# Linear attention of a decoder trunk: the small products gathered into fewer visits between the projections, and four dots moved

## The chip, the core and the metric

The kernel runs on one core of one Trainium2 chip. The metric is device time in microseconds (us) of one execution; three executions of the kernel before are on record. The profile is of one further execution.

## The reference

What is computed is a decoder trunk of two layers on 256 tokens of 1024 channels. The first layer mixes tokens by dilated attention, the second by gated linear attention (the part that matters here); both are followed by a convolutional feed-forward part. Every part gets its input through a root-mean-square norm with a shift and a scale that come from a conditioning vector `c`.

```python
mod = jax.nn.silu(c) @ w_ada[i] + b_ada[i]        # 6 pieces of 1024: shifts, scales, gates
...
q, k, gk = chunks(q, B_DK) * (B_DK ** -0.5), chunks(k, B_DK), chunks(gk, B_DK)   # 4 chunks of 64
q_t = q * jnp.exp(bcum)
k_t = k * jnp.exp(-bcum)
k_d = k * jnp.exp(blast - bcum)
A = jnp.where(causal, jnp.einsum('bhncd,bhnsd->bhncs', q_t, k_t), 0.0)
o_intra = jnp.einsum('bhncs,bhnse->bhnce', A, v)
kv = jnp.einsum('bhncd,bhnce->bhnde', k_d, v)
# scan over the chunks: state = decay * state + kv
o = o_intra + jnp.einsum('bhncd,bhnde->bhnce', q_t, s_prev)
o = rmsnorm(o, g_norm)
return (o * jax.nn.silu(r)) @ w_out
```

There are four heads, with 128 channels of q and k and 256 of v each.

## The kernel before, in words

Channels lie on the 128 partitions and the 256 tokens on the free axis, in 8 tiles `h[kt]` of the normed input. TensorE multiplies in a format of reduced precision, so a projection is split: weights come raw from memory (`split`, L169, issued by SyncE into a pool of four buffers that all weight loads share), ScalarE casts the high part `whi` (L176), VectorE subtracts to get the low part `wlo` (L182), and `mm3` (L203 to L205) makes three products of 128x256 for each tile: high by high, high by low, low by high.

In the linear attention (L1211 on) a head is projected by 8 x 2 x 3 = 48 such products into one bank `pqk`. Then come, for each head:

- VectorE: `k_d`, `q_t`, `k_t` (L1233 to L1235), read from `pqk`.
- TensorE: two transposes of `k_d` into `kdt` (L1241), copied by ScalarE to `kdT` (L1242); the scores `a` from `q_t` and `k_t` (L1252), masked by VectorE into `a_t` (L1253).
- TensorE: three chunk sums `kv`, `kdt`, `kv` of `kdT` with the values `v` (L1265, 64 rows each); from them the states st0 (ScalarE, L1272), st1 and st2 (VectorE, L1274).
- TensorE: the output products `o` from `a_t` and `v` (L1291) and from `q_t` and the states (L1294).
- `normed_output`: squares `osq` by ScalarE (L1301), their sum `oacc` by VectorE (L1303), the mean square `ms` by TensorE (L215), its inverse root by ScalarE (L217, L219), and the scaled output `on` by VectorE (L1308).

These small products are in full single precision. Heads follow each other: while one head is projected, the small products of the head before are put between its projection products. Behind the four heads stand the gate projections `pr` (weights `w_r_b`) and the output projection (`w_out_b`).

The tiles `q_t`, `k_t`, `k_d`, `kdT`, `a_t` and the states have two buffers each: those of the third head take the place of those of the first, and may be written only when the first head's last readers are done. `oacc` and `osq` have one.

The modulation `mod` for the second layer is computed meanwhile by VectorE: `next_ada` (L461) loads one piece of `w_ada` (1 MB) into a buffer of the same pool and makes two dots with `c` (L142, two instructions each: the product with its sum, and the reading of the accumulator). The caller may name instructions behind which the dots are to stand.

The order of each engine's queue is made when the program is built, by a scheduler that goes by estimated times and by the statements `behind(...)`, which say that one instruction is to be issued after another on its engine. Each engine then runs its queue strictly in that order. In the code before, the place of most small products among the projection products is left to the scheduler.

Of the kernel before, what the change touches and what calls it, by code (L numbers as in the profile page):

```python
# [18 lines left out]
P = 128  # L19
D = 1024  # L20
T = 256
# [38 lines left out]
def trunk(ctx: ExitStack, tc: tile.TileContext, I, out):  # L60
# [77 lines left out]
    def ada_dot(l, n, s, raw):  # L138
# [3 lines left out]
        i = nc.vector.tensor_tensor_reduce(  # L142
# [20 lines left out]
    last_load, copied, last_lo = [None], [None], [None]  # L163
# [1050 lines left out]
    def states(hd, between=lambda turned: ()):  # L1214
        if hd == 0:
            w = split(I["w_qk_b"][0][:, KT * P :], KT * P)
            pk = bank("pqk", "p")[:, :T]
            pq = early_q
            for kt in range(KT):
                mm3(pk, parts(w, P * kt), h[kt], kt == 0, kt == KT - 1)  # L1220
        else:
            w = split(I["w_qk_b"][hd], 2048, **(dict(low=first_kt[:1], late=first_kt[:1]) if hd == 2 else {}))
            pqk = bank("pqk", "p")
            pq, pk = pqk[:, :T], pqk[:, T:]
            for kt in range(KT):
                mm3(pq, parts(w, 2 * P * kt), h[kt], kt == 0, False)
                mm3(pk, parts(w, 2 * P * kt + P), h[kt], False, kt == KT - 1)
# [5 lines left out]
        nc.vector.tensor_tensor(k_d, pk, e_d[:, c], op=ALU.mult)  # L1233
        nc.vector.scalar_tensor_tensor(q_t, pq, P ** -0.5, e_q[:, c], op0=ALU.mult, op1=ALU.mult)
        first_kt.append(nc.vector.tensor_tensor(k_t, pk, e_k[:, c], op=ALU.mult))  # L1235

        ps = bank("kdt", "t")
        kd = gt([P, T], "kdT", bufs=2)
        for t in range(2):
            c = slice(P * t, P * t + P)  # L1240
            last_kd = nc.tensor.transpose(ps[:, c], k_d[:, c], ident)  # L1241
        nc.scalar.copy(kd, ps[:, :T])  # L1242

        a_t = gt([P, 2, P], "a_t", bufs=2)
        nc.gpsimd.memset(a_t, 0.0)

        def masked(*after):
            pa = bank("a", "st"[hd == 3])
            for t in range(2):
                c = slice(P * t, P * t + P)  # L1250
                with behind(*after):
                    last_a[0] = mm(pa[:, c], k_t[:, c], q_t[:, c], start=True, stop=True)  # L1252
            kept[0] = nc.vector.copy_predicated(a_t, causal.bitcast(U32), pa[:, :T].rearrange("p (a b) -> p a b", a=2))  # L1253

        if hd < 3:
            masked()
# [238 lines left out]
```

## Time and profile before

| | |
|---|---|
| three executions | 756.5, 756.79, 760.47 us, median 756.79 |
| the profiled execution | 757.08 us |
| its span in the trace | 755.3 us |
| mean granted clock of TensorE | 0.998 |
| dots on VectorE (L142) | 96, 114.3 us busy, 1231 ns each |
| transfers | 187.20 MB, mean 248 GB/s |

Times in the trace are counted from the start of the span. A row of the timeline has the start, the busy time, the engine, the line, the operation, out<-in and the count; in brackets stands the idle time of the engine before it and what released it. One product in full precision counts as two in the trace (a row `x4` can be two instructions). Busy times of neighbouring products overlap, so the time that one costs is read from start to start.

### The profile page before, as it was taken

Reading aid. Unit: us, or ns where it says so; the run is one execution under the profiler, and the core shown is the slowest. Engines: PE = TensorE matmul, PEld = TensorE weight load, DVE = VectorE, ACT = ScalarE, POOL = GpSimd, SP = SyncE. Lnnn points to the kernel's source line nnn. Section 1 sums busy time; section 2 is a strip of 40 time slices with the busy share of each in tenths; the row PEclk is TensorE's granted clock in tenths of the full one; section 3 lists DMA queues with packets and bytes.
Section 4 is the critical chain, followed back from the end, with each engine's and each line's share of the span. In section 5 each row is a group of like instructions: output and inputs, shape, how many; then the busy total and the mean of one; then the engine's idle time right before and its main releaser. Section 6 shows DMA issues by size and latency. Waiting matters only on the chain.

```text
span 755.3 us, 16079 instructions
## 1 busy us (share of the span) xinstructions
PE 746.6 (99%) x6416; PEld 730.4 (97%) x6416; DVE 650.1 (86%) x1197; ACT 483.1 (64%) x949; POOL 32.9 (4%) x57
## 2 busy tenths in 40 slices
PE   8999999999999999999999999999999999999997
PEld 6999999999999999999999999999999999999996
DVE  6999998898889689999999778977959999997592
ACT  5567666566566388676767456925868767666551
POOL 0001010101101010000000000000010000000100
PEclk9999999999999999999999999999999999999999
DMA  9989889879877368777556987854547767774621
GB/s 347 400 298 331 279 311 375 290 233 325 291 250 267 99 222 305 280 261 272 190 183 224 347 272 233 330 224 191 200 169 250 291 216 254 210 174 159 206 98 56
DMA packets 39481, 187.20 MB, mean 248 GB/s; under 512 B 9020, under 2 KB 11708, under 8 KB 25838
## 3 DMA queue, kind: packets, MB, share of 16 engines
q1 hardware_dynamic: 39024, 185.73, 70.2%
q8 instruction: 50, 0.82, 0.4%
q10 hardware_dynamic: 382, 0.45, 0.2%
q14 instruction: 25, 0.20, 0.1%
HBM read 185.06 MB, written 1.10 MB: 246 GB/s over the span
## 4 chain that ended last, share of the span: by engine, by line
PE 90%; DVE 5%; ACT 2%; DMA 2%; issue 1%; DVEq 0%; ACTq 0%
PE pab L204 10%; PE pab L203 10%; PE pab L205 10%; PE pqk L203 6%; PE pqk L205 5%; PE pqk L204 5%; PE pd L204 4%; PE pd L203 4%; PE pd L205 4%; PE pv L203 4%; PE pv L205 4%; PE pv L204 4%; PE py L203 2%; PE py L205 2%; PE py L204 2%; PE early L333 1%
## 5 line engine op out<-in xcount | busy, mean ns | idle before, releaser
L176 ACT CAST whi<-raw 128x1024 fp32r<-128x1024 f32 (+4 forms) x264 | 237.8, 945 | 106.9 <-PE pab L204 54.9
L182 DVE TENSOR_TENSOR wlo<-raw,whi 128x1024 fp32r<-128x1024 f32 (+5 forms) x248 | 263.5, 1093 | 32.2 <-ACT whi L176 31.2
L205 PE MATMUL pab<-hhi,wlo 128*128 128x256 f32 x672 | 184.8, 276 | 0.0
L204 PE MATMUL pab<-hlo,whi 128*128 128x256 f32 x672 | 184.7, 277 | 0.0
L203 PE MATMUL pab<-hhi,whi 128*128 128x256 f32 x672 | 182.9, 277 | 0.0
L204 PEld LDWEIGHTS pab<-hlo,whi 128*128 128x128 f32 x672 | 126.0, 188 | 0.2
L205 PEld LDWEIGHTS pab<-hhi,wlo 128*128 128x128 f32 x672 | 126.2, 188 | 0.0
L203 PEld LDWEIGHTS pab<-hhi,whi 128*128 128x128 f32 x672 | 125.0, 188 | 0.1
L142 DVE CUSTOM_DVE_ANT_0 ada_raw<-ada_raw,c_bc 128x1024 f32<-128x1024 f32 x96 | 114.3, 1231 | 4.2 <-DMA ada_raw<-in_w_ada 4.2
L203 PE MATMUL pqk<-hhi,whi 128*128 128x256 f32 x374 | 102.5, 279 | 0.0
L204 PE MATMUL pqk<-hlo,whi 128*128 128x256 f32 x374 | 102.0, 278 | 0.0
L205 PE MATMUL pqk<-hhi,wlo 128*128 128x256 f32 x374 | 101.5, 278 | 0.0
L205 PE MATMUL pd<-ghi,wlo 128*128 128x256 f32 x308 | 84.9, 276 | 0.0
L204 PE MATMUL pd<-glo,whi 128*128 128x256 f32 x308 | 84.9, 276 | 0.0
L203 PE MATMUL pd<-ghi,whi 128*128 128x256 f32 x308 | 84.7, 276 | 0.0
L203 PEld LDWEIGHTS pqk<-hhi,whi 128*128 128x128 f32 x374 | 69.9, 188 | 0.2
L204 PEld LDWEIGHTS pqk<-hlo,whi 128*128 128x128 f32 x374 | 69.9, 188 | 0.0
L205 PEld LDWEIGHTS pqk<-hhi,wlo 128*128 128x128 f32 x374 | 69.2, 188 | 0.7 <-issue 0.7
L205 PEld LDWEIGHTS pd<-ghi,wlo 128*128 128x128 f32 x308 | 57.8, 188 | 0.0
L204 PEld LDWEIGHTS pd<-glo,whi 128*128 128x128 f32 x308 | 57.8, 188 | 0.0
L203 PEld LDWEIGHTS pd<-ghi,whi 128*128 128x128 f32 x308 | 57.7, 188 | 0.0
L204 PE MATMUL pv<-wlo,hhi 128*128 128x384 f32 (+2 forms) x160 | 52.8, 332 | 0.0
(278 smaller groups left out, 1463.6 us busy)
## 6 DMA issues: line engine op xcount, KB each, us to landing
raw<-in_w_up SPq DMA_DIRECT2D x42, 1024.0 KB, 4.9
ada_raw<-in_w_ada SPq DMA_DIRECT2D x29, 1024.0 KB, 5.9
raw<-in_w_down SPq DMA_DIRECT2D x28, 704.0 KB, 4.4
ada_raw<-in_w_ada SPq DMA_DIRECT2D x38, 512.0 KB, 7.0
raw<-in_wqk SPq DMA_DIRECT2D x18, 1024.0 KB, 6.9
raw<-in_wv SPq DMA_DIRECT2D x14, 768.0 KB, 6.5
raw<-in_w SPq DMA_DIRECT2D x7, 960.0 KB, 5.8
raw<-in_w_v_b SPq DMA_DIRECT2D x6, 768.0 KB, 5.7
```

The costliest lines, as they stand in the source:

```text
L142: i = nc.vector.tensor_tensor_reduce(w, w, c_bc, op0=ALU.mult, op1=ALU.add, scale=1.0, scalar=0.0, accum_out=dot,)
L176: copied[0] = nc.scalar.copy(part(hi[:, c]), part(raw[:, c]))
L182: last_lo[0] = nc.vector.tensor_tensor(part(lo[:, c]), part(raw[:, c]), part(hi[:, c].bitcast(F32)), op=ALU.subtract)
L203: mm(ps, a[0], b[0], start=start, stop=False)
L204: mm(ps, a[0], b[1], start=False, stop=False)
L205: return mm(ps, a[1], b[0], start=False, stop=stop)
L333: mm(ps[:, 0 : T + 1], early[:, P * kt : P * kt + P], early_x[kt][:, 0 : T + 1], start=(kt == 0), stop=(kt == KT - 1))
```

## The change

The function `states` is taken apart into its steps (`head`, `project_head`, `scaled_head`, `turned_head`, `masked_head`, `sums_of_head`, `states_of_head`, `products`), and the main sequence now calls the steps in the order in which TensorE is to run them, each behind the one before. Between halves (four of the eight tiles) of the third and fourth heads' projections stand four visits of small products: transposes and scores of the first head; its sums; transposes and scores of the second head; and the second head's sums with the third head's transposes and the first head's output products. The rest follows the fourth head's projection. The two pieces of `w_ada` that were taken behind the first and second gates are now taken together behind the third head's `k_t`, ahead of the fourth head's projection in the program; the second head's st1 and st2 are stated to stand behind their dots.

All 148 rows of TensorE in the stretch from the third head's projection to the gates are the same instructions in another order. The returns from small products to projection products in it go from nine to five. First, TensorE before, in the fourth head's projection (`pqk`); `kv` and `kdt` are the chunk sums of the second head, `o` an output product of the first. The first sum stands by itself:

```order
L204 MATMUL pqk<-hlo,whi 128x256
L1265 MATMUL kdt<-v_6365,kdT 128x256
L205 MATMUL pqk<-hhi,wlo 128x256
...
L205 MATMUL pqk<-hhi,wlo 128x256
L203 MATMUL pqk<-hhi,whi 128x256
L1265 MATMUL kv<-v_6365,kdT 128x256
L1265 MATMUL kv<-v_6366,kdT 128x256
L1294 MATMUL o<-q_t,st_6689 128x64
L204 MATMUL pqk<-hlo,whi 128x256
```

Behind the change (lines of the new code: sums L1280, transposes L1256, output products L1307 and L1310) the three sums stand together at the half of the fourth head, with the third head's transposes and the first head's output products right behind:

```order
L205 MATMUL pqk<-hhi,wlo 128x256
L1280 MATMUL kv<-v_6365,kdT 128x256
L1280 MATMUL kdt<-v_6365,kdT 128x256
L1280 MATMUL kv<-v_6366,kdT 128x256
L1256 MATMUL kdt<-ident,k_d 128x128 x2
L1307 MATMUL o<-a_t,v_6365 128x128
L1310 MATMUL o<-q_t,st_6783 128x64
L1307 MATMUL o<-a_t,v_6366 128x128
L1310 MATMUL o<-q_t,st_6785 128x64
L1310 MATMUL o<-q_t,st_6787 128x64
```

What moved: the sums are in one piece, and all ten output products of the first head, which before were spread over the projection, stand directly behind them. Next, the end of the fourth head's projection after the change. `ms` is the mean square of the first head's output, `a` the third head's scores, the sums those of the third head:

```order
L205 MATMUL pqk<-hhi,wlo 128x256
L215 MATMUL ms<-oacc,ones_d 128x256
L1268 MATMUL a<-q_t,k_t 128x128 x2
L1280 MATMUL kv<-v_6365,kdT 128x256
L1280 MATMUL kdt<-v_6365,kdT 128x256
L1280 MATMUL kv<-v_6366,kdT 128x256
```

Before, `ms` stood behind the third head's sums; now it stands directly behind the last projection product, ahead of them. On VectorE before, around `q_t` of the third head (`q_t_6858`); `st1_6773` is the second head's, `oacc_6790` the first head's. No dot is among these rows; one pair stands directly ahead of them and another some rows further ahead:

```order
L1233 TENSOR_TENSOR k_d_6860<-pqk_6809,e_d_6547 128x256
L1274 SCALAR_TENSOR_TENSOR st2_6691<-st1_6689,dec_6531,kv_6683 128x256
L1274 SCALAR_TENSOR_TENSOR st1_6773<-st0_6771,dec_6553,kdt_6756 128x256
L1274 SCALAR_TENSOR_TENSOR st2_6775<-st1_6773,dec_6553,kv_6767 128x256
L1234 SCALAR_TENSOR_TENSOR q_t_6858<-pqk_6809,e_q_6548 128x256
L1235 TENSOR_TENSOR k_t_6859<-pqk_6809,e_k_6549 128x256
L1303 TENSOR_TENSOR oacc_6790<-osq_6788 128x256
L1233 TENSOR_TENSOR k_d_6944<-pqk_6893,e_d_6547 128x256
```

VectorE after, from `q_t` of the third head (`q_t_6833`), which is the instruction that waits for TensorE's output products of the first head, to `oacc` of the first head (`oacc_6937`):

```order
L1245 SCALAR_TENSOR_TENSOR q_t_6833<-pqk_6737,e_q_6548 128x256
L1246 TENSOR_TENSOR k_t_6834<-pqk_6737,e_k_6549 128x256
L142 ISA ada_raw_6839,dot_6841<-ada_raw_6839,c_bc_97 128x1024
L142 ISA dot_6841 128x1
L142 ISA ada_raw_6839,dot_6845<-ada_raw_6839,c_bc_97 128x1024
L142 ISA dot_6845 128x1
L142 ISA ada_raw_6849,dot_6851<-ada_raw_6849,c_bc_97 128x1024
L142 ISA dot_6851 128x1
L142 ISA ada_raw_6849,dot_6855<-ada_raw_6849,c_bc_97 128x1024
L142 ISA dot_6855 128x1
L1292 SCALAR_TENSOR_TENSOR st1_6889<-st0_6887,dec_6553,kdt_6822 128x256
L1319 TENSOR_TENSOR oacc_6937<-osq_6935 128x256
```

Four dots (eight rows) now stand between `k_t` of the third head and st1 of the second head, and so ahead of the first head's `oacc`. SyncE's queue of loads before and after, from the last weights of q and k on (`w_r_b` are the gate weights):

```order
L169 DMA raw<-in_w_qk_b 128x2048 x3
L169 DMA raw<-in_w_r_b 128x2048
L135 DMA ada_raw<-in_w_ada 128x2048
L169 DMA raw<-in_w_r_b 128x2048
L135 DMA ada_raw<-in_w_ada 128x2048 x2
```

```order
L169 DMA raw<-in_w_qk_b 128x2048 x3
L135 DMA ada_raw<-in_w_ada 128x2048 x2
L169 DMA raw<-in_w_r_b 128x2048 x2
L135 DMA ada_raw<-in_w_ada 128x2048
L169 DMA raw<-in_w_r_b 128x2048
```

Both moved pieces of `w_ada` now stand ahead of the first gate weights.

The diff, with the new functions:

```diff
@@ -139,7 +139,7 @@
-        i = nc.vector.tensor_tensor_reduce(
+        i = dotted[0] = nc.vector.tensor_tensor_reduce(
...
@@ -1211,81 +1211,97 @@
     o_n, first_kt, accs = [], [], []
     last_a, last_sq, copies, kept = [None], [None], [None], [None, None]
 
-    def states(hd, between=lambda turned: ()):
+    heads = [{} for _ in range(4)]
+
+    def head(hd, **kw):
+        y = heads[hd]
         if hd == 0:
-            w = split(I["w_qk_b"][0][:, KT * P :], KT * P)
-            pk = bank("pqk", "p")[:, :T]
-            pq = early_q
-            for kt in range(KT):
-                mm3(pk, parts(w, P * kt), h[kt], kt == 0, kt == KT - 1)
+            y["w"] = split(I["w_qk_b"][0][:, KT * P :], KT * P)
+            y["pq"], y["pk"] = early_q, bank("pqk", "p")[:, :T]
         else:
-            w = split(I["w_qk_b"][hd], 2048, **(dict(low=first_kt[:1], late=first_kt[:1]) if hd == 2 else {}))
+            y["w"] = split(I["w_qk_b"][hd], 2048, **kw)
             pqk = bank("pqk", "p")
-            pq, pk = pqk[:, :T], pqk[:, T:]
-            for kt in range(KT):
-                mm3(pq, parts(w, 2 * P * kt), h[kt], kt == 0, False)
-                mm3(pk, parts(w, 2 * P * kt + P), h[kt], False, kt == KT - 1)
+            y["pq"], y["pk"] = pqk[:, :T], pqk[:, T:]
+
+    def project_head(hd, kts, *after):
+        y = heads[hd]
+        for kt in kts:
+            with behind(*after):
+                if hd:
+                    mm3(y["pq"], parts(y["w"], 2 * P * kt), h[kt], kt == 0, False)
+                    last = mm3(y["pk"], parts(y["w"], 2 * P * kt + P), h[kt], False, kt == KT - 1)
+                else:
+                    last = mm3(y["pk"], parts(y["w"], P * kt), h[kt], kt == 0, kt == KT - 1)
+        return last
+
+    def scaled_head(hd):
+        y = heads[hd]
         part = min(hd, 1)
         e_q, e_k, e_d, dec = gates[part]
         own = hd - PARTS[part][0]
         c = slice(T * own, T * own + T)
         q_t, k_t, k_d = (gt([P, T], nm, bufs=2) for nm in ("q_t", "k_t", "k_d"))
-        nc.vector.tensor_tensor(k_d, pk, e_d[:, c], op=ALU.mult)
-        nc.vector.scalar_tensor_tensor(q_t, pq, P ** -0.5, e_q[:, c], op0=ALU.mult, op1=ALU.mult)
-        first_kt.append(nc.vector.tensor_tensor(k_t, pk, e_k[:, c], op=ALU.mult))
-
-        ps = bank("kdt", "t")
-        kd = gt([P, T], "kdT", bufs=2)
+        nc.vector.tensor_tensor(k_d, y["pk"], e_d[:, c], op=ALU.mult)
+        nc.vector.scalar_tensor_tensor(q_t, y["pq"], P ** -0.5, e_q[:, c], op0=ALU.mult, op1=ALU.mult)
+        first_kt.append(nc.vector.tensor_tensor(k_t, y["pk"], e_k[:, c], op=ALU.mult))
+        y.update(q_t=q_t, k_t=k_t, k_d=k_d, dec=dec[:, 4 * own : 4 * own + 4])
+
+    def turned_head(hd, *after):
+        y = heads[hd]
+        y["ps"] = ps = bank("kdt", "t")
+        y["kd"] = kd = gt([P, T], "kdT", bufs=2)
         for t in range(2):
             c = slice(P * t, P * t + P)
-            last_kd = nc.tensor.transpose(ps[:, c], k_d[:, c], ident)
+            with behind(*after):
+                last = nc.tensor.transpose(ps[:, c], y["k_d"][:, c], ident)
         nc.scalar.copy(kd, ps[:, :T])
-
-        a_t = gt([P, 2, P], "a_t", bufs=2)
-        nc.gpsimd.memset(a_t, 0.0)
-
-        def masked(*after):
-            pa = bank("a", "st"[hd == 3])
-            for t in range(2):
-                c = slice(P * t, P * t + P)
-                with behind(*after):
-                    last_a[0] = mm(pa[:, c], k_t[:, c], q_t[:, c], start=True, stop=True)
-            kept[0] = nc.vector.copy_predicated(a_t, causal.bitcast(U32), pa[:, :T].rearrange("p (a b) -> p a b", a=2))
-
-        if hd < 3:
-            masked()
+        y["a_t"] = gt([P, 2, P], "a_t", bufs=2)
+        nc.gpsimd.memset(y["a_t"], 0.0)
+        return last
+
+    def masked_head(hd, *after):
+        y = heads[hd]
+        pa = bank("a", "st"[hd == 3])
+        for t in range(2):
+            c = slice(P * t, P * t + P)
+            with behind(*after):
+                last_a[0] = mm(pa[:, c], y["k_t"][:, c], y["q_t"][:, c], start=True, stop=True)
+        kept[0] = nc.vector.copy_predicated(y["a_t"], causal.bitcast(U32), pa[:, :T].rearrange("p (a b) -> p a b", a=2))
+        return last_a[0]
+
+    def sums_of_head(hd, *after):
+        y = heads[hd]
         vh = slice(T * hd, T * hd + T)
-        st = []
-        ahead = between(last_kd)
         kv = bank("kv", "t")
+        y["d"] = kv[:, :T], y["ps"][:, T:], kv[:, T:]
         for n in range(3):
             t, r = n // 2, slice(CH * (n % 2), CH * (n % 2) + CH)
-            d = (kv[:, :T], ps[:, T:], kv[:, T:])[n]
-            with behind(*ahead):
-                last = mm(d, kd[r, P * t : P * t + P], v[t][r, vh], start=True, stop=True)
-        if hd == 3:
-            masked(last)
+            with behind(*after):
+                last = mm(y["d"][n], y["kd"][r, P * t : P * t + P], v[t][r, vh], start=True, stop=True)
+        return last
+
+    def states_of_head(hd, *after):
+        y = heads[hd]
+        st = []
         for n in range(3):
-            d = (kv[:, :T], ps[:, T:], kv[:, T:])[n]
             s = gt([P, T], f"st{n}", bufs=2)
             if n == 0:
-                copies[0] = nc.scalar.copy(s, d)
+                copies[0] = nc.scalar.copy(s, y["d"][n])
             else:
-                kept[1] = nc.vector.scalar_tensor_tensor(s, st[-1], dec[:, 4 * own + n : 4 * own + n + 1], d,
-                                               op0=ALU.mult, op1=ALU.add)
+                with behind(*after):
+                    kept[1] = nc.vector.scalar_tensor_tensor(s, st[-1], y["dec"][:, n : n + 1], y["d"][n],
+                                                             op0=ALU.mult, op1=ALU.add)
             st.append(s)
-        return q_t, a_t, st
+        y["state"] = y["q_t"], y["a_t"], st
 
     last_o = [None]
 
-    def output(hd, *state):
-        normed_output(hd, products(hd, *state))
-
-    def products(hd, q_t, a_t, st, last=None):
+    def products(hd, *after):
+        q_t, a_t, st = heads[hd]["state"]
         po = bank("o", "s")
         for et in range(2):
             ev = slice(T * hd + P * et, T * hd + P * et + P)
-            with behind(*([last] if last and et else [])):
+            with behind(*after):
                 for t in range(2):
                     d = po[:, T * et + P * t : T * et + P * t + P]
                     mm(d, v[t][:, ev], a_t[:, t, :], start=True, stop=False)
@@ -1330,23 +1346,46 @@
             with behind(*norm_ops[1:]):
                 nc.scalar.activation(r_g[-1], pr, AF.Silu)
 
-    s0 = states(0)
-    s1 = states(1)
-    output(0, *s0)
-    s2 = states(2)
-    po1 = []
-
-    def ahead(turned):
-        po1.append(products(1, *s1, last=turned))
-        return last_o
-
-    s3 = states(3, ahead)
-    normed_output(1, po1[0], last_a)
-    po2 = products(2, *s2)
+    head(0)
+    project_head(0, range(KT))
+    scaled_head(0)
+    head(1)
+    last = project_head(1, range(KT))
+    head(2, low=first_kt[:1], late=first_kt[:1])
+    turned_head(0, last)
+    last = masked_head(0, last)
+    scaled_head(1)
+    last = project_head(2, range(4), last)
+    last = sums_of_head(0, last)
+    states_of_head(0)
+    head(3, low=first_kt[1:2], late=first_kt[1:2])
+    last = project_head(2, range(4, KT), last)
+    turned_head(1, last)
+    last = masked_head(1, last)
+    scaled_head(2)
+    for _ in range(2):
+        next_ada(kept[0], first_kt[2])
+    last = project_head(3, range(4), last)
+    last = sums_of_head(1, last)
+    states_of_head(1, dotted[0])
+    last = turned_head(2, last)
+    po0 = products(0, last)
+    last = project_head(3, range(4, KT), last_o[0])
+    normed_output(0, po0, [last])
+    last = norm_ops[0]
+    scaled_head(3)
+    masked_head(2, last)
+    last = sums_of_head(2, last)
+    states_of_head(2)
+    last = turned_head(3, last)
+    po1 = products(1, last)
+    last = sums_of_head(3, last_o[0])
+    masked_head(3, last)
+    states_of_head(3)
+    normed_output(1, po1, last_a)
+    po2 = products(2)
     gate(0)
-    low_0 = last_lo[0]
-    next_ada(first_kt[1])
-    po3 = products(3, *s3)
+    po3 = products(3)
     normed_output(2, po2, last_o)
     normed_output(3, po3)
 
@@ -1357,7 +1396,6 @@
             for s in range(2):
                 nc.scalar.copy(level[kt][s], h[kt][s])
     gate(1)
-    next_ada(low_0)
     next_ada(accs[2])
     for n in range(4):
 
```

More of the change, by code (lines that the diff above doesn't have):

```diff
@@ L160, in ada_chunk @@
                 ada_dot(l, n, s, raw)
-    last_load, copied, last_lo = [None], [None], [None]
+    last_load, copied, last_lo, dotted = [None], [None], [None], [None]
     def split(src, n, dmas=1, after=((), ()), late=(), low=(), lows=True, view=None):
```

## The prediction

> **What bounds the kernel now.** I read the page first: busy time of the engines, then the shares of the chain that ended last.
>
> ```profile
> PE 746.6 (99%) x6416; PEld 730.4 (97%) x6416; DVE 650.1 (86%) x1197; ACT 483.1 (64%) x949; POOL 32.9 (4%) x57
> PE 90%; DVE 5%; ACT 2%; DMA 2%; issue 1%; DVEq 0%; ACTq 0%
> ```
>
> TensorE (PE) is busy for 99% of the span. So a time saved on PE is a time saved, and a time in which PE waits is added; work elsewhere counts only where PE comes to wait for it. Second, the stretch that the change rewrites, from the projection of the third head to the gates, as busy time by stretch (the columns are the stretch, its length, busy us and counts of PE, PEld, DVE, ACT and POOL, then the granted clock, the DMA share and GB/s).
>
> ```profile
> 491.40:498.20 6.80, 6.80 (x57) 6.29 (x56) 6.80 (x11) 2.18 (x5) 0.00 (x0) 1.00 0.60 226
> 498.20:509.60 11.40, 11.40 (x90) 10.38 (x88) 7.59 (x16) 2.76 (x8) 0.31 (x1) 1.00 0.63 235
> 509.60:518.60 9.00, 9.00 (x69) 7.83 (x67) 6.23 (x14) 5.16 (x9) 0.31 (x1) 1.00 0.00 1
> ```
>
> PE has no gap in these 27.2 us, at the full clock. There is no PE wait here that a better order could remove; only the price of switching between kinds of product can go. VectorE (DVE) has slack: 11.40 − 7.59 = 3.8 us in the second stretch and 2.8 us in the third. Third, what DVE waits for there, by its timeline; the last row has the wait in brackets.
>
> ```profile
> 496.37 1.22 DVE L142 CUSTOM_DVE_ANT_0 ada_raw<-ada_raw,c_bc 128x1024 f32<-128x1024 f32 x1
> 498.66 1.22 DVE L182 TENSOR_TENSOR wlo<-raw,whi 128x1024 fp32r<-128x1024 f32 x1
> 508.43 0.42 DVE L1234 SCALAR_TENSOR_TENSOR q_t<-pqk,e_q 128x256 f32<-128x256 f32 x1 [2.40 <-PE o L1294]
> 508.77 0.41 DVE L1235 TENSOR_TENSOR k_t<-pqk,e_k 128x256 f32<-128x256 f32 x1
> 509.10 0.42 DVE L1303 TENSOR_TENSOR oacc<-osq 128x256 f32<-128x256 f32 x1
> ```
>
> The third row is the most important of all. It is q_t of the third head. That tile has two buffers, so it may be written only after the output products of the first head, its last readers, are done. DVE waited 2.40 us for them with nothing in hand. The dots (one pair began at 496.37, and the next work followed at 498.66, so a pair takes 2.29 us) stood ahead of this wait, where DVE had time to spare.
>
> **The change part by part. (1) Fewer returns to the projection: −1.1.** All 96 projection products and all small products remain; only their order differs. Rows of PE in the stretch (start, busy, line):
>
> ```profile
> 492.02 0.37 PE L203 MATMUL pqk<-hhi,whi 128*128 128x256 f32 x1
> 492.23 0.28 PE L204 MATMUL pqk<-hlo,whi 128*128 128x256 f32 x1
> 492.35 0.28 PE L205 MATMUL pqk<-hhi,wlo 128*128 128x256 f32 x1
> ...
> 501.06 0.28 PE L204 MATMUL pqk<-hlo,whi 128*128 128x256 f32 x1
> 501.27 0.70 PE L1265 MATMUL kdt<-v,kdT 64*128 64x256 f32 x2
> 501.90 0.38 PE L205 MATMUL pqk<-hhi,wlo 128*128 128x256 f32 x1
> 502.12 0.28 PE L203 MATMUL pqk<-hhi,whi 128*128 128x256 f32 x1
> 502.24 0.28 PE L204 MATMUL pqk<-hlo,whi 128*128 128x256 f32 x1
> ```
>
> The first projection product behind a visit takes 0.21 us until the next one starts, against 0.12 in a run of them: a return costs 0.09. The chunk sums of the second head stand in two pieces. The one-product piece occupies PE from 501.18 (501.06 and a regular step of 0.12) to 501.90, and its return takes 0.22 instead of 0.12: 0.72 + 0.10 = 0.82. That the sums in one visit cost no more than the remaining piece of two is read from the first head, whose three stand together:
>
> ```profile
> 495.29 0.28 PE L204 MATMUL pqk<-hlo,whi 128*128 128x256 f32 x1
> 495.50 0.48 PE L1265 MATMUL kv<-v,kdT 64*128 64x256 f32 x1
> ...
> 496.56 0.39 PE L205 MATMUL pqk<-hhi,wlo 128*128 128x256 f32 x1
> ...
> 503.18 0.28 PE L203 MATMUL pqk<-hhi,whi 128*128 128x256 f32 x1
> 503.39 1.13 PE L1265 MATMUL kv<-v,kdT 64*128 64x256 f32 x4
> 504.45 0.43 PE L1294 MATMUL o<-q_t,st 128*128 128x64 f32 x2
> ```
>
> Three of them: 495.29 to 496.56, 1.27. The two left over in the second head: 503.18 to 504.45, 1.27 as well. So the single piece is saved whole, 0.82. In the order of instructions the returns to the projection fall from nine to five; one of the four is in the piece, and three more give 3 × 0.09 = 0.27. Together −1.1. The bounds are 0 (the joined visits put other switches in their place) and −1.5 (each of the four visits saves its way in as well).
>
> **(2) The four dots behind k_t of the third head: +3.6.** Afterwards DVE has, in this order: q_t of the third head (still waiting for the first head's output products), k_t, two pairs of dots, st1 of the second head, oacc of the first. PE now has the output products directly behind the second head's sums, then the second half of the fourth head's projection, and then ms, the mean square made from that oacc. The third head's scores, sums, the output products of the second head and everything behind are queued behind ms. So the chain from the end of the first head's output products to ms decides, and its length comes from these rows and those above:
>
> ```profile
> 508.23 0.39 PE L1241 MATMUL kdt<-ident,k_d 128*128 128x128 f32 x2
> 512.35 0.47 DVE L1274 SCALAR_TENSOR_TENSOR st<-st,dec,kv 128x256 f32<-128x256 f32 x1
> 512.73 0.87 DVE L1308 SCALAR_TENSOR_TENSOR on<-o,small,rstd 128x256 f32<-128x256 f32 x2
> 514.85 0.41 DVE L1235 TENSOR_TENSOR k_t<-pqk,e_k 128x256 f32<-128x256 f32 x1
> 515.46 0.71 PE L1252 MATMUL a<-q_t,k_t 128*128 128x128 f32 x4
> ```
>
> PE left the output products at 508.23 and q_t began at 508.43: 0.20. q_t to k_t 0.34, k_t to the next 0.33. Two pairs of dots 2 × 2.29 = 4.58. st1 0.38 (512.35 to 512.73). oacc 0.42, and from the end of a DVE result to the PE product on it 0.20 (k_t ends at 515.26, the scores start at 515.46). The sum is 0.20 + 0.34 + 0.33 + 4.58 + 0.38 + 0.42 + 0.20 = 6.45 us. In that time PE has 24 projection products. 48 of them ran from
>
> ```profile
> 485.99 0.28 PE L203 MATMUL pqk<-hhi,whi 128*128 128x256 f32 x1
> ...
> 491.44 0.38 PE L1241 MATMUL kdt<-ident,k_d 128*128 128x128 f32 x2
> ```
>
> in 5.45 us, so 24 take 2.72, with the return 2.81. PE stands still for 6.45 − 2.81 = 3.6 us. Without the dots it would not: 6.45 − 4.58 = 1.87 is less than 2.81. The bounds of this stall are 3.0 (the hops shorter, DVE's operations closer together) and 4.0 (st1 or the first squares on ScalarE late by some tenths). DVE waits longer before q_t in turn, since it has no dots to fill that time (2.40 + 4.58, less some 2 us by which the output products come earlier: about 5), but nothing on PE is late for it: q_t and k_t are first needed by the third head's scores, which stand behind ms anyway.
>
> **(3) Loads.** The two ada loads move ahead of the gate weights on SyncE's queue, so the first gate weights take a later slot.
>
> ```profile
> 492.92 0.33 SPq L169 DMA_DIRECT2D raw<-in_w_r_b  x1
> raw<-in_w_r_b SPq DMA_DIRECT2D x4, 1024.0 KB, 6.4
> 532.44 2.00 ACT L176 CAST whi<-raw 128x1024 fp32r<-128x1024 f32 x2
> ```
>
> A slot like that of 492.92 with the median of 6.4 us to landing gives 499.3. ScalarE's casts of 1 us a half stand ahead of its copy of the second head's kdT, which the joined sums need at about 502 to 503. That is hidden; with a landing two us later some tenths would show. I take 0, bounds 0 and +0.3. The third and fourth gate loads start when the dots free their buffers, some 10 us before PE uses them, and stay hidden.
>
> **(4) The tail of the stretch.** The mean square of the third head joins another visit and saves about 0.1, which I leave out; the casts of the first output weights stand behind a table load on ScalarE and shorten a slack of about 2 us there: 0, bound +1.
>
> **The sum.** The profiled execution took 757.08 us (span 755.3): 757.08 − 1.1 + 3.6 = 759.6. It lies 0.29 above the median of the runs shown, 756.79, so the forecast for the median is **759.3 us**, 0.33% above before. The likeliest case's own range, with the bounds of its terms (−1.5 + 3.0 at one end; 0.3 less saved and 4.0 at the other), is 758.3 to 760.0.
>
> **The rivals. (a) The clock falls in the new stall, slower than before.** At the end of the program PE goes idle:
>
> ```profile
> 749.08 0.85 PE L916 MATMUL y<-ident,x_all 128*128 128x128 f32 x6
> 749.00:752.00 3.00, 0.94 (x9) 0.69 (x8) 1.73 (x5) 1.45 (x4) 0.00 (x0) 0.96 0.00 0
> 752.00:755.00 3.00, 0.00 (x0) 0.00 (x0) 0.00 (x0) 0.00 (x0) 0.00 (x0) 0.50 0.45 175
> ```
>
> The last product ends at 749.93. The clock averages 0.96 up to 752 and is 0.50 after it, so it fell (1 − 0.96) × 3.00 / 0.50 = 0.24 us ahead of 752, that is 1.8 us after the last product. A stall of 3.6 us is twice that. What it costs to come back is seen at the start, where the same warming products take 2.08 / 8 = 0.26 us each and later 1.16 / 8 = 0.145:
>
> ```profile
> 6.65 2.08 PE L301 MATMUL warm<-ones_d 128*128 128x128 f32 x8
> 10.64 1.05 PE L301 MATMUL warm<-ones_d 128*128 128x128 f32 x6
> 13.01 1.16 PE L301 MATMUL warm<-ones_d 128*128 128x128 f32 x8
> ```
>
> The slow spell lasts from 6.65 to about 11, at most 4.4 us at about half rate: a loss of at most 2.2; part of it can pass while PE still stands still. I take +1.5, so 760.8, 0.5% slower, with 761.5 as its far end. The place is the small products behind ms, and it decides only if the stall exceeds 1.8 us. Against it speaks that a single fall, at the program's end, is all that these rows hold. The Trainium skill, page "TensorE: Matmul & The Clock Gate", section "What's actually happening", says that the gate falls to half rate after at least one idle window of about 3.4 us, and that windows run freely. By that rule a stall of 3.6 us would seldom hold a whole window, and the sum would stay at 759.3; the row of 1.8 us does not fit a whole idle window, so the trace so far leans the other way. Chance 0.33.
>
> **(b) The dots are hidden.** If ms or oacc does not wait behind the dots (a wait falls elsewhere than I read), only term (1) is left: 756.79 − 1.1 = 755.7. For it: DVE has 3.8 us of slack in the stretch. Against it: that slack lies in waits ahead of q_t, and the dots stand behind it in a queue that runs in order. Chance 0.09.
>
> **(c) The change also stalls the output projection** by using up the slack of part (4): +0.9, so 760.2. Chance 0.08.
>
> **How the numbers follow.** The forecast has the remaining 0.50. The range 758.2 to 761.4 takes in the forecast, (c) and nearly all of (a); outside lie (b) and some of the tail of (a). A measurement of this kernel can tell about 0.5%, 3.8 us, from no change: 753.0 and 760.6 are the borders. Slower than 760.6: two thirds of (a), a quarter of (c) and a few of the forecast's misses, with the unknown size of a lower clock in mind 0.30. Faster than 753.0 would take a gain that no row shows: 0.02. Within: 0.68.
>
> **What would show it.** In the profile after, the waits of PE should have ms waiting for oacc, some 3.6 us, in a stretch that had none; DVE's wait for q_t by the output products should grow from 2.4 to about 5; the four dots should stand back to back behind k_t; the granted clock at the small products behind ms tells forecast from (a). The stretch without its stall should be about 1.1 us shorter. I am wrong if PE has no gap at ms, if the gap is there but shorter than 3 us, or if a new gap appears at the gate weights.

## The result and the profile after

The changed kernel takes 765.58 us (median of six executions, 761.75 to 770.01), against 756.75 us for the kernel before (756.5 to 760.47): a ratio of 1.0109, 95% interval 1.0072 to 1.0146. Measured again beside the experiments on another occasion it took 766.29 us against 757.14 us, 1.0119 (1.0089 to 1.0149). The profiled execution took 765.64 us, its span is 763.8 us.

The page of the changed kernel, first the engines, then the granted clock by slice of 19.1 us:

```profile
PE 752.2 (98%) x6416; PEld 734.9 (96%) x6416; DVE 650.9 (85%) x1197; ACT 483.7 (63%) x949; POOL 33.1 (4%) x57
...
PEclk9999999999999999999999999987999999999999
```

DVE, ACT and POOL have as much to do as before. TensorE has 5.6 us more of busy time for the same instructions, and two slices have a clock under 0.9, where before no slice had. Both lie in the stretch that the change rewrites. The waits of TensorE in it, in one row (us in all, times, longest), and TensorE's timeline there:

```profile
PE ms L215 <- DVE oacc L1319: 3.4, 1, 3.4
```

```profile
504.89 0.56 PE L1310 MATMUL o<-q_t,st 128*128 128x64 f32 x4
505.25 0.37 PE L203 MATMUL pqk<-hhi,whi 128*128 128x256 f32 x1
...
508.05 0.28 PE L205 MATMUL pqk<-hhi,wlo 128*128 128x256 f32 x1
511.69 1.19 PE L215 MATMUL ms<-oacc,ones_d 128*128 128x256 f32 x2 [3.36 <-DVE oacc L1319]
512.68 1.06 PE L1268 MATMUL a<-q_t,k_t 128*128 128x128 f32 x4
...
523.47 1.06 PE L215 MATMUL ms<-oacc,ones_d 128*128 128x256 f32 x2
524.33 0.57 PE L1307 MATMUL o<-a_t,v 128*128 128x128 f32 x2
...
526.30 0.56 PE L1310 MATMUL o<-q_t,st 128*128 128x64 f32 x4
526.66 0.37 PE L203 MATMUL pr<-hhi,whi 128*128 128x256 f32 x1
```

The stall is where the prediction put it: 3.36 us at ms of the first head, for oacc. Behind it every product takes nearly twice its time from start to start until 524 us; by busy time the scores take 1.06 instead of 0.61 and ms 1.19 instead of 0.7. VectorE in the same place:

```profile
499.46 0.44 DVE L1269 COPY_PREDICATED a_t<-causal,a 128x256 f32<-128x256 uint32 x1
505.48 0.42 DVE L1245 SCALAR_TENSOR_TENSOR q_t<-pqk,e_q 128x256 f32<-128x256 f32 x1 [5.59 <-PE o L1310]
505.82 0.41 DVE L1246 TENSOR_TENSOR k_t<-pqk,e_k 128x256 f32<-128x256 f32 x1
506.15 1.22 DVE L142 CUSTOM_DVE_ANT_0 ada_raw<-ada_raw,c_bc 128x1024 f32<-128x1024 f32 x1
...
510.73 0.48 DVE L1292 SCALAR_TENSOR_TENSOR st<-st,dec,kdt 128x256 f32<-128x256 f32 x1
511.13 0.42 DVE L1319 TENSOR_TENSOR oacc<-osq 128x256 f32<-128x256 f32 x1
```

VectorE stands idle for 5.59 us at q_t, and then has 4.58 us of dots (506.15 to 510.73) ahead of the oacc that TensorE waits for. The stretch cut at the places where the clock changes (columns as before: length, busy us of PE, PEld, DVE, ACT and POOL, granted clock, DMA share, GB/s):

```profile
490.70:508.30 17.60, 17.60 (x144) 16.40 (x142) 10.64 (x18) 4.00 (x9) 0.31 (x1) 1.00 0.32 121
508.30:511.05 2.75, 0.03 (x1) 0.00 (x0) 2.75 (x7) 1.07 (x4) 0.00 (x0) 1.00 0.49 140
511.05:511.70 0.65, 0.01 (x1) 0.04 (x1) 0.65 (x3) 0.19 (x1) 0.00 (x0) 0.50 1.07 454
511.70:524.71 13.01, 13.01 (x48) 10.64 (x49) 5.23 (x14) 4.38 (x8) 0.31 (x1) 0.50 0.26 109
524.71:526.66 1.95, 1.95 (x20) 1.95 (x19) 1.95 (x2) 1.95 (x4) 0.00 (x0) 1.00 0.00 0
```

The clock fell to 0.50 at 511.05, 2.7 us after TensorE's last product had ended at 508.33, and came back at 524.71. From the first transpose at the start of the stretch to the first gate product it now takes 526.66 - 490.70 = 35.96 us; before it took 518.59 - 491.44 = 27.15. That is 8.81 us more: 3.4 from the stall and some 6.2 from 13 us of work at half clock, less 0.8 by which the stretch is shorter without a stall (experiments 1 and 8 to 10 size the last two). What lies ahead of the stretch is 0.74 us shorter and what lies behind it 0.5 longer in this execution, which leaves the 8.6 us of the two profiled executions.

### The profile page after: what moved, and what is told of

Its sections match the earlier page's. It is cut to its first block, busy times and chain, and to the rows that moved or that the text cites. A ratio compares the mean times of both kernels' runs of the same rounds, so it can differ in the third digit from the quotient of the medians.

```text
span 763.8 us, 16078 instructions
## 1 busy us (share of the span) xinstructions
PE 752.2 (98%) x6416; PEld 734.9 (96%) x6416; DVE 650.9 (85%) x1197; ACT 483.7 (63%) x949; POOL 33.1 (4%) x57
## 4 chain that ended last, share of the span: by engine, by line
PE 89%; DVE 5%; DMA 3%; ACT 2%; issue 1%; SPq 0%; DVEq 0%; ACTq 0%
PE pab L204 10%; PE pab L203 10%; PE pab L205 10%; PE pqk L203 5%; PE pqk L205 5%; PE pqk L204 5%; PE pd L204 4%; PE pd L205 4%; PE pd L203 4%; PE pv L205 4%; PE pv L203 4%; PE pv L204 4%; PE py L203 2%; PE py L205 2%; PE py L204 2%; DVE ada_raw L142 2%
```

## The experiments

Each experiment is set against the kernel before on the same chip: experiments 1 to 4 on one chip, 5 to 8 on a second, 9 to 11 on a third. Theory A: the four dots hold back oacc, TensorE stands still for it, and in that stall the clock falls; the order of TensorE's products itself is harmless. Rival B: the order itself (small full-precision products packed together) or the earlier loads slow TensorE. Rival C: four dots are too much for this stretch wherever they stand.

**1. The dots ahead of q_t**, TensorE's order and the loads as in the change.

```diff
-    scaled_head(2)
     for _ in range(2):
-        next_ada(kept[0], first_kt[2])
+        next_ada(kept[0], first_kt[1])
+    scaled_head(2)
```

> The new order of TensorE is kept whole; only the four dots are taken ahead of q_t of the third head, into the wait that VectorE has there anyway. Theory A (the dots hold back oacc, TensorE stands still at ms for 3.4 us, and the granted clock falls in that stall): no wait of TensorE at ms, the clock stays at 1.00, and only the saved returns are left: 756.75 - 1.1 = 755.7 us. Rival B (the order itself is to blame: the small full-precision products packed together, or the earlier loads, bring the clock down or slow the products): the time stays near 765 us with no stall.

Measured: 756.15 us against 757.07 us, 0.999 (0.998 to 1.0). On VectorE the dots now fill the wait, and TensorE runs from the projection into ms:

```profile
505.34 0.48 DVE L1292 SCALAR_TENSOR_TENSOR st<-st,dec,kdt 128x256 f32<-128x256 f32 x1
...
506.32 0.42 DVE L1245 SCALAR_TENSOR_TENSOR q_t<-pqk,e_q 128x256 f32<-128x256 f32 x1
...
506.98 0.42 DVE L1319 TENSOR_TENSOR oacc<-osq 128x256 f32<-128x256 f32 x1
```

```profile
508.55 0.28 PE L205 MATMUL pqk<-hhi,wlo 128*128 128x256 f32 x1
508.67 0.59 PE L215 MATMUL ms<-oacc,ones_d 128*128 128x256 f32 x2
```

The last dot ends before st1 at 505.34, oacc is done at 507.40, 1.3 us ahead of ms. Same order on TensorE, same order of loads, no stall, full clock: rival B falls. The stretch takes 26.38 us (491.06 to 517.44), 0.77 less than before: that is what the new order saves there.

**2. One pair of dots ahead of q_t, one behind k_t.**

```diff
+    next_ada(kept[0], first_kt[1])
     scaled_head(2)
-    for _ in range(2):
-        next_ada(kept[0], first_kt[2])
+    next_ada(kept[0], first_kt[2])
```

> One pair of dots ahead of q_t of the third head, the other pair left where the change put both, behind k_t. Theory A: the wait at ms shrinks by one pair, 3.4 - 2.3 = 1.1 us. If the clock falls only when the idle time goes on for over 1.8 us, it stays at 1.00 here, and the time is 755.7 + 1.1 = 756.8 us. If any wait of about 1 us is enough for the clock to fall, half-clock time of one or more spells is added, 758.5 to 763. Rival B: near 765 us.

Measured: 757.81 us, 1.0016 (0.9999 to 1.0033). The wait at ms:

```profile
PE ms L215 <- DVE oacc L1319: 1.1, 1, 1.1
```

3.36 - 2.29 = 1.07 us, as expected: the stall goes with the number of dots ahead of oacc. The clock stayed at 1.00 through it. The median is 1.0 us above the 756.8 expected; the stretch of the profiled execution is 27.55 us, 1.17 more than in experiment 1, so the rest lies outside it and was not followed up.

**3. The stall filled with products of no use.** Eleven small products of a constant tile go into the bank of ms ahead of the real one; they add work and change no result.

```diff
-    def rstd_of(squares, n=D, tag=None):
+    def rstd_of(squares, n=D, tag=None, idle=0):
         ps = bank("ms", tag)
+        for _ in range(idle):
+            mm(ps[:, :P], ones_d, ones_d, start=True, stop=True)
...
-            rr = rstd_of([acc], 256, "s")
+            rr = rstd_of([acc], 256, "s", 11 if hd == 0 else 0)
```

> The changed kernel with its dots where the change put them, plus eleven 128x128 products of a constant tile on TensorE, directly ahead of the ms of the first head and written into the bank that ms then overwrites: about 11 x 0.29 = 3.2 us of work of no use in a stall of 3.4 us. Theory A: ms starts when it did (VectorE is as late as before), but TensorE is not idle, the clock stays at 1.00, and the time is 755.7 + 3.4 = 759.1 us; the difference from the changed kernel, some 6 us, is the price of the clock alone. Rival B: unchanged, near 765 us, with the clock low again.

Measured: 760.03 us, 1.0048 (1.0031 to 1.0066). TensorE idles for 0.81 us instead of 3.36, and ms starts no earlier:

```profile
508.71 2.62 PE L215 MATMUL ms<-ones_d 128*128 128x128 f32 x22
512.14 0.70 PE L217 MATMUL ms<-oacc,ones_d 128*128 128x256 f32 x2 [0.81 <-DVE oacc L1321]
512.68 0.61 PE L1270 MATMUL a<-q_t,k_t 128*128 128x128 f32 x4
```

The scores take 0.61 us again: the clock is full. This separates the two costs. The wait as such is worth 760.03 - 756.15 = 3.9 us by the medians, and 29.78 - 26.38 = 3.4 us by the stretches of experiments 3 (491.24 to 521.02) and 1. The clock is worth 766.29 - 760.03 = 6.3 us in the median of the changed kernel's later measurement; counted from the kernel before on its own chip, 9.15 - 2.96 = 6.2.

**4. Three buffers for q_t**, so that it waits for nobody.

```diff
-        q_t, k_t, k_d = (gt([P, T], nm, bufs=2) for nm in ("q_t", "k_t", "k_d"))
+        q_t, k_t, k_d = (gt([P, T], nm, bufs=3 if nm == "q_t" else 2) for nm in ("q_t", "k_t", "k_d"))
```

> The changed kernel with three buffers for q_t instead of two, nothing else edited. q_t of the third head need not wait for the output products of the first, so q_t, k_t and the four dots start some 5.6 us earlier, and oacc is not late. Theory A: no wait of TensorE at ms, clock at 1.00, 755.7 us, the same as with the dots moved ahead. If instead the dots are too long wherever they stand in this stretch (4.6 us of VectorE's time are not there), a wait of 1 us or more remains at ms or at the third head's products.

Measured: 756.49 us, 0.9988 (0.9976 to 0.9999), with no wait of TensorE in the stretch. The dots stand behind k_t, as in the change, yet start early, since q_t is not held:

```profile
501.30 0.41 DVE L1245 SCALAR_TENSOR_TENSOR q_t<-pqk,e_q 128x256 f32<-128x256 f32 x1
...
502.30 1.22 DVE L142 CUSTOM_DVE_ANT_0 ada_raw<-ada_raw,c_bc 128x1024 f32<-128x1024 f32 x1
...
507.89 0.42 DVE L1319 TENSOR_TENSOR oacc<-osq 128x256 f32<-128x256 f32 x1
```

So the cause has two conditions, the dots and the wait ahead of them: dots behind a waiting instruction cost, the same dots behind one that does not wait do not. Rival C falls.

**5. The kernel before with the dots alone moved**, TensorE's order left to the scheduler.

```diff
             w = split(I["w_qk_b"][hd], 2048, **(dict(low=first_kt[:1], late=first_kt[:1]) if hd == 2 else {}))
+            if hd == 3:
+                for _ in range(2):
+                    next_ada(first_kt[2])
...
-    low_0 = last_lo[0]
-    next_ada(first_kt[1])
...
-    next_ada(low_0)
```

> The kernel before with only the dots moved: both pieces of w_ada behind k_t of the third head, loads ahead of the gate weights as in the change, and TensorE's order left to the scheduler. The scheduler then puts oacc of the first head ahead of the dots and the first head's output products earlier. Theory A (what costs is oacc queued behind dots while ms stands at TensorE's head, not the dots as such): no wait of TensorE over 1 us, clock at 1.00, 756 to 758 us. Rival C (four dots in this stretch or the moved loads are themselves too much): some 3 us of waits and a time over 760 us.

Measured: 755.97 us, 0.9989 (0.9975 to 1.0003), no wait of TensorE in the stretch. The scheduler then puts oacc ahead of the dots by itself, takes the sums of the second head in one visit, and the stretch takes 26.09 us, 0.29 less than with the order stated by hand in experiment 1. It moved a good deal of TensorE's order with the dots, so it shows that the moved dots and loads do no harm there, not what they cost in the old order. It also shows that a stretch as short does not need the new order.

**6. Five products of no use instead of eleven** (the edit of experiment 3 with 5 for 11).

> As the run with eleven products of no use ahead of ms, but five of them: 1.2 us of work, so that TensorE is idle for about 2.2 us in one piece instead of 0.8. It asks how long an idle time lets the clock fall. Without a fall 760.0 us as with eleven. If 1.8 us is enough whatever came before, the clock falls in most executions and the time is 762 to 766 us. If it needs over 2.2 us, or depends on where a free-running window stands, none or a part of the executions is slower, with their mean clock below 0.997.

Measured: 761.96 us, 1.0067 (1.0047 to 1.0088), six executions from 759.18 to 764.13. The wait of the profiled one:

```profile
511.93 0.70 PE L217 MATMUL ms<-oacc,ones_d 128*128 128x256 f32 x2 [2.15 <-DVE oacc L1321]
```

Four of the six have a mean clock of 0.995 to 0.997, two of 0.998 and 1.0; no execution of the kernel before measured beside them is under 0.998. By the mean clock, then, an idle time of 2.15 us lets the clock fall in a part of the executions; only the profiled one has a trace, and in it the clock did not fall. Its windows, shown with experiments 8 to 10, say why.

**7. ms ahead of the second half of the projection**, which makes the stall as long as the whole chain and puts projection products behind it.

```diff
-    last = project_head(3, range(4, KT), last_o[0])
-    normed_output(0, po0, [last])
-    last = norm_ops[0]
+    normed_output(0, po0, [last_o[0]])
+    last = project_head(3, range(4, KT), norm_ops[0])
     scaled_head(3)
```

> The changed kernel, but TensorE's ms of the first head stands ahead of the second half of the fourth head's projection instead of behind it. The stall grows to the whole chain, 6.3 us, and what follows it is 24 projection products and not small ones. The clock must fall. It asks what ends the slow spell. If each free-running window of 3.41 us full of work ends it, the spell is 2 or 3 such windows, 1.7 to 3.4 us are lost to it, and the time is 755.9 + 6.3 + 1.7 to 3.4 = 764 to 765.6 us. If the spell is always four windows (13.65 us, as in the profile of the changed kernel), 4.5 to 6 us are lost: 767 to 768 us.

Measured: 764.32 us, 1.0096 (1.008 to 1.0112), stall 6.25 us: the case of two or three windows. The stall is longer by 2.9 us, yet the median is no longer than the change's 766.29 (762.29 to 771.2). The slow spell is three windows long, and TensorE works in it for only 2.46 + 3.41 = 5.9 us, against 13 in the change's first profile:

```profile
504.51:507.92 3.41, 1.54 (x15) 1.40 (x13) 1.84 (x5) 0.60 (x1) 0.31 (x1) 1.00 0.00 0
507.92:511.34 3.42, 0.00 (x0) 0.00 (x0) 3.42 (x9) 1.36 (x5) 0.00 (x0) 0.50 0.35 81
511.34:514.75 3.41, 2.46 (x9) 2.31 (x10) 1.47 (x6) 1.28 (x3) 0.00 (x0) 0.50 1.00 408
514.75:518.16 3.41, 3.41 (x18) 3.41 (x17) 0.60 (x2) 0.00 (x0) 0.00 (x0) 0.50 0.31 125
```

The first of these rows ends with the fall; the last is full of projection products and ends with the clock's return at 518.16.

**8 to 10. The changed kernel three times more, 11. experiment 7 once more**, for the spells.

> The changed kernel once more, beside the others on one chip, for the spread of its executions. Theory A: the stall is 3.4 us in each, and the spread comes from the number of windows at half clock: the mean clock of an execution goes with its time, at about 0.5 us for each us at half clock, from 760 us with one or two windows to 766 with four or five. Rival: the times spread without regard to the clock.

> The changed kernel again, one profiled execution, to see another spell at half clock. On the grid of 3.41 us windows found in the runs so far (a window with at most 1.74 us of TensorE idle kept the clock, one with at least 1.83 us lost it), the stall of 3.4 us puts over 1.8 us of idle into one window unless the grid cuts it nearly in the middle, so the clock should fall at the end of that window. The length should be a whole number of windows, 1 to 4 as seen.

> As the run before, one more execution with another place of the grid: a fall at the end of the window that holds over 1.8 us of idle, and a spell of a whole number of windows. If every spell behind a first one of 4 windows and one of 1 window has one of these two lengths, the length goes with the place of the grid in the small products.

> The run with ms ahead of the projection once more. If a window full of projection products always ends the spell, the clock is back at the end of the first window that holds only such products, as it was at 518.16 us in the run before: 2 or 3 windows in all.

Experiments 9 to 11 are one execution each (765, 764.33 and 767.62 us, the kernel before 758.28). The stall at ms is 3.36 us in all four profiled executions of the change. What differs is the spell at half clock. The trace records when the granted clock changed; the time between two changes is a whole number of 3.413 us: 217 of them from the first rise to the fall at the end of the kernel before (740.69 us), and 4, 1, 2 and 3 for the spells of the change. With the time from ms of the first head to the first gate product:

| execution | windows at half clock | ms to gate, us | more than in experiment 1 |
|---|---|---|---|
| experiment 1 | 0 | 8.77 | |
| experiment 8 | 1 | 10.46 | 1.7 |
| experiment 9 | 2 | 12.04 | 3.3 |
| experiment 10 | 3 | 13.66 | 4.9 |
| the change's first profile | 4 | 14.97 | 6.2 |

Each window costs 1.6 to 1.7 us, half of its length (the first of the four held 0.64 us of the stall). Experiment 10 asked whether every spell has either 1 or 4 windows; 2 and 3 came too. On this grid the fall can be read too. Experiment 10, its windows around the stall (the busy time of PE stands first):

```profile
506.67:510.09 3.42, 1.85 (x16) 1.65 (x14) 3.42 (x7) 1.06 (x4) 0.00 (x0) 1.00 0.24 34
510.09:513.50 3.41, 1.61 (x11) 1.42 (x12) 2.77 (x7) 1.55 (x5) 0.00 (x0) 1.00 0.87 356
513.50:516.91 3.41, 3.41 (x16) 2.76 (x14) 1.88 (x5) 0.76 (x3) 0.00 (x0) 0.50 0.54 226
```

The grid cuts the stall nearly in the middle. The first window has 1.57 us idle and is followed by full clock, the second has 1.80 idle, and the clock falls at its end, though TensorE had been at work again for 1.6 us. In experiment 8 one window holds 2.14 us of the stall and loses the clock, and the next, full of small products, brings it back:

```profile
509.77:513.18 3.41, 1.27 (x8) 1.13 (x10) 2.76 (x9) 1.40 (x5) 0.00 (x0) 1.00 0.90 324
513.18:516.60 3.42, 3.42 (x15) 2.60 (x14) 2.23 (x5) 1.11 (x3) 0.00 (x0) 0.50 0.70 280
```

Experiment 6, whose clock did not fall, and the window at the end of the change's first profile that still kept the clock:

```profile
507.64:511.05 3.41, 2.14 (x19) 1.95 (x17) 3.41 (x7) 1.36 (x5) 0.00 (x0) 1.00 0.36 74
511.05:514.47 3.42, 2.54 (x16) 1.99 (x17) 2.84 (x9) 1.58 (x4) 0.00 (x0) 1.00 0.98 407
```

```profile
756.82:760.23 3.41, 1.67 (x16) 1.43 (x14) 1.73 (x5) 1.45 (x4) 0.00 (x0) 1.00 0.10 37
```

They hold 1.27, 0.88 and 1.74 us of idle time. In all eleven experiments and both first profiles, each window with up to 1.74 us of idle kept the clock and each with 1.80 or more lost it (outside spells): the point lies between 51% and 53% of a window, as far as the ends of products, which are modelled, can be trusted to some hundredths. Experiment 11 had two windows at half clock, the second full of projection products, as expected; its stretch began 3 us later than in experiment 7.

The six executions of experiment 8 answer theory A in part: 762.29 and 763.44 us come with a mean clock of 0.997 and 0.999, and 766.18 to 766.71 us with 0.990 and 0.991, so the clock parts these two groups. But the sixth, 771.2 us, has 0.990 as well. The kernel before also has executions some 3 us above its median at a full clock (759.8 and 760.36 us at 0.999), so a part of the spread is not the clock's; its cause was not looked for.

## Why the prediction was wrong

The forecast was 759.3 us, its range 758.2 to 761.4; the time is 765.58.

- **The path and the stall were right.** Term (2) said that the chain from the output products to ms takes 6.45 us and the stall 3.6: TensorE left the output products at 505.25 and began ms at 511.69, 6.44 us, and the recorded stall is 3.36. It is smaller because it counts from the end of the last projection product at 508.33, and because these products came every 0.118 us instead of 0.114. VectorE's longer wait at q_t, about 5, is 5.59.
- **Term (1) was mis-sized a little**: -1.1 forecast, -0.77 in the stretch of experiment 1, where nothing else is in the way. Its projection products follow each other at 0.117 us, against 0.115 before (the mean of 88 and of 82 steps inside a run of them): some 0.2 us of the 0.33. What causes that was not tried.
- **Terms (3) and (4) were right.** The first gate weights' cast waited 1.2 us for its load and held up nothing; no stall appeared behind the stretch.
- **The step that failed is the price of the stall: the sum counted its length alone and put the clock at nothing, and rival (a), which held the clock, had too small a chance and too small a price.** It was a case of 0.33 at +1.5 us, with at most 4.4 us at half clock. It happened in every profiled execution of the change, and cost 1.7, 3.3, 4.9 and 6.2 us. Without it, experiment 3 stands at 760.03 us, 0.7 from the forecast. A part of that nearness is luck: the stall came out 0.24 shorter and the saving 0.33 smaller, and the two nearly cancel.

The chance was too low because the row of 1.8 us stood alone, and I gave it less than an even chance against a rule. I also read that row as a delay behind the last product. It is not one: in the change's first profile the clock fell 2.7 us after the last product, and in experiment 8, 4.6 us after. What counts is the idle time inside one window of the grid, and the window of the kernel before that ended with the fall (748.36 to 751.77) held 1.84 us of it; that the delay came out so near to this is luck of the grid's place in that execution.

The Trainium skill, page "TensorE: Matmul & The Clock Gate", section "What's actually happening", says that windows of about 3.4 us run freely and that the clock is low after at least one idle window. The first point agrees with the traces, whose changes of the clock lie whole multiples of 3.413 us apart. On the second the measurement decides otherwise: 1.80 us of idle in a window is enough. With that, a stall of 3.36 us keeps the clock only if the grid cuts it so that neither part reaches 1.8 us, that is with a part between 1.56 and 1.8 us. If every place of the grid is as likely, that is 0.24 / 3.41 = 7% of the places, by my estimate. One untraced execution of the change (763.44 us at a mean clock of 0.999) may be such a one.

The price was wrong because I took the slow spell from the program's start, one spell of unlike work. The same section of the Trainium skill says that a busy window brings the full clock back. That holds for a window full of projection products (514.75 to 518.16 in experiment 7, 517.05 to 520.46 in experiment 11). It does not always hold for the small full-precision products that follow the stall here: in the first profile two windows in which TensorE was busy throughout did not bring it back, and the third did:

```profile
514.47:517.88 3.41, 3.41 (x15) 2.67 (x14) 1.54 (x4) 0.74 (x2) 0.00 (x0) 0.50 0.18 74
517.88:521.30 3.42, 3.42 (x17) 3.21 (x17) 0.74 (x3) 0.60 (x1) 0.31 (x1) 0.50 0.00 0
521.30:524.71 3.41, 3.41 (x12) 2.49 (x11) 1.75 (x6) 2.15 (x3) 0.00 (x0) 0.50 0.00 0
```

In experiment 8 the first such window did, in experiment 9 the second, in experiment 10 the third. What in a window of small products decides was not found: neither its count of products nor the weight loads' busy time (2.67 and 3.21 did not, 2.49 did) sorts the cases, nor whether transposes are among them (517.88 to 521.30 has none and failed, the window of experiment 8 has them and did not). That stays open.

The change itself is two parts that meet badly. Its order of TensorE gains 0.8 us in the stretch (though experiment 5 gets 1.1 with another order); its place for the dots loses 3.4 + 6.2 = 9.6 us in the profiled execution, because an instruction that waits stands ahead of them and the one that TensorE needs behind them. With the dots ahead of q_t (experiment 1, 756.15 against 757.07) or with a third buffer (experiment 4), the new order is as fast as the kernel before or slightly faster: 0.6 to 0.9 us in the median, which the 95% intervals barely part from nothing.

## What to carry to other kernels

Work put behind a waiting instruction on an in-order engine does not fill the wait; it lengthens the chain behind it. Only work ahead of the wait is free (the same four dots: 756.15 us ahead of q_t, 765.58 behind it). So count the chain from the wait's release to the next instruction that the bounding engine needs. On TensorE a new stall has two prices, its length and the clock. As soon as it can put about 1.8 us of idle into one window of 3.4, reckon with a fall: here four of six executions had one at 2.15 us, by their mean clock, and all four profiled ones at 3.36. Then add 1.7 us for each window at half clock, one to four of them here where small full-precision products followed. When the stall can't be removed, fill it: eleven products of no use saved 6 us.

## What the hardware showed that was not expected

In all thirteen profiled executions the granted clock changed only on a grid of 3.413 us, at the end of a window, whose place differs from execution to execution. So it can fall when TensorE is already back at work: in experiment 8 it fell at 513.18, 1.3 us after ms had begun, for the 2.14 us of idle at the window's start. The length of the following spell, 1 to 4 windows with the same instructions, alone moves the time from ms to the gates from 10.46 to 14.97 us. That is much of the spread of the changed kernel's times (761.75 to 771.2 us), but not all of it: the executions of 770.01 and 771.2 us have the same mean clock, 0.990, as those of 766.18 to 766.71.

A stall nearly twice as long (6.25 us, experiment 7) took no more time in the median than one of 3.36. That it cost less is not shown: its stretch takes 35.33 us, and 35.03 in experiment 11, against 31.45 to 35.96 in the four profiled executions of the change. What is shown is that less work ran at half clock behind it than in the change's first profile, 5.9 us against 13.
